# A row-normalizing kernel: the fourth load's last row and the first store's lead in 4 KB packets

## The chip, the cores and the metric

The kernel runs on one core of a Trainium2 chip. The metric is the device time of one execution in microseconds (us); the median over several runs is compared. VectorE is called DVE in the profile, ScalarE ACT, SyncE SP; "ACTq" and "SPq" are the instruction queues in which ACT and SP issue DMAs. The core has 16 DMA engines, and a DMA is cut into packets that are spread over them.

## The reference

```python
batch, seq, dim = 32, 512, 1024
x = np.random.randn(batch, seq, dim).astype(np.float32)

sums = np.sum(np.abs(x), axis=-1, keepdims=True)
out = (x / (sums + 1e-8)).astype(np.float32)
```

Each of the 32 x 512 = 16384 rows of 1024 float32 values is divided by the sum of its absolute values. The input is 67.11 MB and so is the output; every byte is read once and written once.

## The kernel before

The 16384 rows are spread over 128 partitions, 128 rows on each, and cut into 11 tiles. Tiles 0, 1 and 10 come from the first 4096 rows, where each partition owns 32 rows in a run (12, 12 and 8 of them); each of tiles 2 to 9 is a block of 1536 rows, 12 rows in a run per partition. A row is 4 KB, so a tile of 12 rows has 48 KB per partition and 6 MB in all; tile 10 has 4 MB. Four buffers (`BUFS = 4`) hold the tiles in turn, and everything is done in place in them.

For each tile `normalize` runs on DVE: a reduction of absolute values for all rows (line 47), the addition of the epsilon (54), the reciprocal (56). Then the rows are scaled in three groups, set by `split`: the first `kv` rows in one broadcast multiply on DVE (58), the next `kt` rows one by one on DVE (65), the last rows one by one on ACT (68). For tile 0 `split` is (3, 4): 5 rows in the broadcast multiply, 3 single ones on DVE, 4 on ACT.

The order is written out by hand (`manual_schedule`): SP issues loads 0 to 3; then for each tile come the computation, its store, and the load of the tile four further on. Loads go through SP's DMA queue (q1 in the profile, line 87) and stores through ACT's (q10, line 97). Load i+4 needs the buffer of tile i, so SP waits for the end of store i before it issues it; behind that wait stand only later loads. Tiles wait for one another in nothing else but the order on each engine.

`max_dma_last_dim` sets the packet size: it cuts the run of each partition into pieces. Loads 0 and 1 go in pieces of 48 KB (`WHOLE`), the others in halves of the run. Store 0 is two DMAs: rows 0 to 2 (`FIRST = 3`) in packets of one row, 4 KB, which waits for the broadcast multiply alone, then rows 3 to 11 in one packet of 36 KB per partition, which waits for all of tile 0. Store 8 is two DMAs too. The other stores are one DMA each, in packets of 24 KB, 48 KB (tile 9) or 32 KB (tile 10).

Of the kernel before, what the change touches and what calls it, by code (L numbers as in the profile page):

```python
# [1 line left out]

# [4 lines left out]

FP32 = mybir.dt.float32
EPS = 1e-8


@with_exitstack
def kernel(
    ctx: ExitStack,
    tc: tile.TileContext,
    x: bass.AP,
    out: bass.AP,
):
    nc = tc.nc
    P = nc.NUM_PARTITIONS  # L20

    x_flat = x.flatten_outer_dims()
    out_flat = out.flatten_outer_dims()
    n, d = x_flat.shape

    R = 12
    BUFS = 4
    HEAD = 32
    per_partition = n // P
    assert n % P == 0 and (per_partition - HEAD) % R == 0  # L30
    rows = [R] * ((per_partition - HEAD) // R + 2) + [HEAD - 2 * R]

    def piece(flat, i):
        head = flat[: P * HEAD, :].rearrange("(p r) d -> p r d", p=P)
        if i < 2:
            return head[:, R * i : R * (i + 1), :]
        if i == len(rows) - 1:
            return head[:, 2 * R :, :]
        a = P * (HEAD + R * (i - 2))
        return flat[a : a + P * R, :].rearrange("(p r) d -> p r d", p=P)  # L40

    sbuf = ctx.enter_context(tc.tile_pool(name="sbuf", bufs=BUFS))
    stats = ctx.enter_context(tc.tile_pool(name="stats", bufs=len(rows)))

    def normalize(x_tile, k, kv, kt):
        s = stats.tile([P, R], FP32)
        nc.vector.tensor_reduce(  # L47
            out=s[:, :k],
            in_=x_tile[:, :k, :],
            axis=mybir.AxisListType.X,  # L50
            op=mybir.AluOpType.add,
            apply_absolute_value=True,
        )
        nc.vector.tensor_scalar_add(out=s[:, :k], in0=s[:, :k], scalar1=EPS)  # L54
        inv = stats.tile([P, R], FP32)
        nc.vector.reciprocal(out=inv[:, :k], in_=s[:, :k])  # L56
        if kv:
            nc.vector.tensor_mul(  # L58
                out=x_tile[:, :kv, :],
                in0=x_tile[:, :kv, :],  # L60
                in1=inv[:, :kv].unsqueeze(2).to_broadcast([P, kv, d]),
            )
        for r in range(kv, kv + kt):
            row = x_tile[:, r, :]
            nc.vector.tensor_scalar_mul(out=row, in0=row, scalar1=inv[:, r : r + 1])  # L65
        for r in range(kv + kt, k):
            row = x_tile[:, r, :]
            nc.scalar.activation(  # L68
                out=row,
                in_=row,  # L70
                func=mybir.ActivationFunctionType.Copy,
                scale=inv[:, r : r + 1],
            )

    last = len(rows) - 1
    split = {0: (3, 4), 1: (0, 3), 2: (0, 3), last - 1: (0, 2), last: (4, 4)}

    tiles = {}

    HALF, WHOLE = 24576, 49152
    FIRST = 3

    def load(i):
        x_tile = tiles[i] = sbuf.tile([P, R, d], FP32, name="x_tile")
        nc.sync.dma_start(out=x_tile[:, : rows[i], :], in_=piece(x_flat, i), max_dma_last_dim=WHOLE if i < 2 else HALF)  # L87

    def store(i):
        if i == 0:  # L90
            parts = [(0, FIRST, 4 * d), (FIRST, R, WHOLE)]
        elif i == last - 2:
            parts = [(0, R // 2, HALF), (R // 2, R, HALF)]
        else:
            parts = [(0, rows[i], WHOLE if i >= last - 1 else HALF)]
        for a, b, size in parts:
            nc.scalar.dma_start(
                out=piece(out_flat, i)[:, a:b, :],
                in_=tiles[i][:, a:b, :],
                max_dma_last_dim=size,  # L100
            )

    def compute(i):
        k = rows[i]
        kt, ks = split.get(i, (0, 0))
        normalize(tiles[i], k, k - kt - ks, kt)

    with tc.manual_schedule():
        for i in range(BUFS):
            load(i)  # L110
        for i in range(len(rows)):
            compute(i)
            store(i)
            if i + BUFS < len(rows):
                load(i + BUFS)


# [1 line left out]
_INS = ['x']  # L119
_OUTS = [((32, 512, 1024), 'float32')]  # L120


# [23 lines left out]
```

## Time and profile before

| | |
|---|---|
| median of 3 runs | 316.62 us (316.51 to 316.66) |
| span of the profiled execution, first to last instruction | 315.2 us (315.155 in the trace) |
| median less the span | 1.46 us |
| DVE busy | 260.6 us (83%) |
| ACT busy | 18.5 us (6%) |
| moved by DMA | 134.22 MB in 5761 packets, 426 GB/s over the span |
| first packet of a load, last packet of a store | 1.73 us, ends at 313.83 us |
| first part of store 0 issued | 36.78 us |
| load 3 landed, store 0 ended | 65.86 us, 76.76 us |
| load 4 issued | 76.83 us |
| last store issued | 293.25 us |

The page gives the span of the profiled execution and no other time for it; the runs that the median comes from lie 1.46 us above this span. Times in the table, and all that are given as a moment, count from the start of the span. A packet's record in the trace holds its start, its duration, its size and its queue. The DMA row of the page gives the busy share of the 16 DMA engines in 40 equal slices, each digit a tenth.

### The profile page before, as it was taken

Reading aid. Unit: us, or ns where it says so; the run is one execution under the profiler, and the core shown is the slowest. Engines: PE = TensorE matmul, PEld = TensorE weight load, DVE = VectorE, ACT = ScalarE, POOL = GpSimd, SP = SyncE. Lnnn points to the kernel's source line nnn. Section 1 sums busy time; section 2 is a strip of 40 time slices with the busy share of each in tenths; the row PEclk is TensorE's granted clock in tenths of the full one; section 3 lists DMA queues with packets and bytes.
Section 4 is the critical chain, followed back from the end, with each engine's and each line's share of the span. In section 5 each row is a group of like instructions: output and inputs, shape, how many; then the busy total and the mean of one; then the engine's idle time right before and its main releaser. Section 6 shows DMA issues by size and latency. Waiting matters only on the chain.

```text
span 315.2 us, 172 instructions
## 1 busy us (share of the span) xinstructions
DVE 260.6 (83%) x50; ACT 18.5 (6%) x17; POOL 0.2 (0%) x4
## 2 busy tenths in 40 slices
DVE  0079999999999999989996997999699969999000
ACT  0010503004000000000000000000000000203200
POOL 0000000000000000000000000000000000000000
DMA  8999999999999999999999999999999999999997
GB/s 318 480 399 412 437 407 464 411 436 413 415 446 437 415 446 437 415 449 434 415 449 437 412 449 437 412 449 437 415 446 437 415 437 434 432 428 496 399 408 324
DMA packets 5761, 134.22 MB, mean 426 GB/s; under 512 B 385, under 2 KB 385, under 8 KB 769
## 3 DMA queue, kind: packets, MB, share of 16 engines
q1 hardware_dynamic: 2736, 67.11, 49.8%
q10 hardware_dynamic: 3024, 67.11, 49.4%
q14 instruction: 1, 0.00, 0.0%
HBM read 67.11 MB, written 67.11 MB: 426 GB/s over the span
## 4 chain that ended last, share of the span: by engine, by line
DVE 40%; DMA 33%; another core or an unknown queue 18%; ACT 1%; issue 0%; SPq 0%
DVE s L47 23%; DMA x_tile<-in_x_dram 17%; DMA out_dram<-x_tile 16%; DVE x_tile L58 15%; ACT x_tile L68 1%; DVE x_tile L65 1%; DVE inv L56 0%; DVE s L54 0%; SPq L87 0%
## 5 line engine op out<-in xcount | busy, mean ns | idle before, releaser
L47 DVE TENSOR_REDUCE s<-x_tile 128x12 f32<-128x12288 f32 (+1 forms) x11 | 138.2, 12562 | 29.8 <-DMA x_tile<-in_x_dram 29.8
L58 DVE TENSOR_TENSOR x_tile<-x_tile,inv 128x12288 f32<-128x12288 f32 (+3 forms) x10 | 113.6, 11358 | 0.5
L68 ACT ACTIVATE x_tile<-x_tile,inv 128x1024 f32<-128x1024 f32 x16 | 17.2, 1138 | 256.9 <-DVE inv L56 256.9
L65 DVE TENSOR_SCALAR x_tile<-x_tile,inv 128x1024 f32<-128x1024 f32 x7 | 4.8, 749 | 0.0
L56 DVE RECIPROCAL inv<-s 128x12 f32<-128x12 f32 (+1 forms) x11 | 2.5, 226 | 0.4
L68 ACT ACT_TABLE_LOAD x1 | 1.3, 1283 | 17.8 <-DMA x_tile<-in_x_dram 17.8
L54 DVE TENSOR_SCALAR s<-s 128x12 f32<-128x12 f32 (+1 forms) x11 | 1.9, 174 | 0.4
L130 POOL MEMSET const-bfloat16-1.0<- 128x1 bf16 x1 | 0.1, 101 | 0.0
L130 POOL MEMSET const-uint8-127<- 128x1 uint8 x1 | 0.1, 101 | 0.0
L130 POOL MEMSET const-float32-0.0<- 128x1 f32 x1 | 0.1, 98 | 0.2 <-issue 0.2
L130 POOL MEMSET const-float32-1.0<- 128x1 f32 x1 | 0.1, 98 | 0.0
## 6 DMA issues: line engine op xcount, KB each, us to landing
x_tile<-in_x_dram SPq DMA_DIRECT2D x10, 6144.0 KB, 36.9
out_dram<-x_tile ACTq DMA_DIRECT2D x8, 6144.0 KB, 49.1
out_dram<-x_tile ACTq DMA_DIRECT2D x2, 3072.0 KB, 33.4
out_dram<-x_tile ACTq DMA_DIRECT2D x1, 4608.0 KB, 37.9
x_tile<-in_x_dram SPq DMA_DIRECT2D x1, 4096.0 KB, 32.2
out_dram<-x_tile ACTq DMA_DIRECT2D x1, 4096.0 KB, 20.9
out_dram<-x_tile ACTq DMA_DIRECT2D x1, 1536.0 KB, 29.3
```

The lines of the kernel that those rows point to most:

```text
L47: nc.vector.tensor_reduce(out=s[:, :k], in_=x_tile[:, :k, :], axis=mybir.AxisListType.X, op=mybir.AluOpType.add, apply_absolute_value=True,)
L54: nc.vector.tensor_scalar_add(out=s[:, :k], in0=s[:, :k], scalar1=EPS)
L56: nc.vector.reciprocal(out=inv[:, :k], in_=s[:, :k])
L58: nc.vector.tensor_mul(out=x_tile[:, :kv, :], in0=x_tile[:, :kv, :], in1=inv[:, :kv].unsqueeze(2).to_broadcast([P, kv, d]),)
L65: nc.vector.tensor_scalar_mul(out=row, in0=row, scalar1=inv[:, r : r + 1])
L68: nc.scalar.activation(out=row, in_=row, func=mybir.ActivationFunctionType.Copy, scale=inv[:, r : r + 1],)
L130: nc = _bacc.Bacc("TRN2", target_bir_lowering=False, num_devices=1)
```

## The change

Load 3, the last of the loads that are issued at the start, becomes two DMAs: rows 0 to 10 in two packets of 22 KB per partition, and row 11 (`TAIL = 1`) in one packet of 4 KB per partition. The first part of store 0 gets four rows in 4 KB packets instead of three (`FIRST = 4`), and its second part eight rows in one packet of 32 KB per partition instead of nine in one of 36 KB. So that the first part still waits for the broadcast multiply alone, tile 0's `split` goes from (3, 4) to (2, 4): 6 rows in the broadcast multiply, 2 single ones on DVE, 4 on ACT. Nothing else changes.

```diff
     last = len(rows) - 1
-    split = {0: (3, 4), 1: (0, 3), 2: (0, 3), last - 1: (0, 2), last: (4, 4)}
+    split = {0: (2, 4), 1: (0, 3), 2: (0, 3), last - 1: (0, 2), last: (4, 4)}
...
     HALF, WHOLE = 24576, 49152
-    FIRST = 3
+    FIRST = 4
+    TAIL = 1
 
     def load(i):
         x_tile = tiles[i] = sbuf.tile([P, R, d], FP32, name="x_tile")
-        nc.sync.dma_start(out=x_tile[:, : rows[i], :], in_=piece(x_flat, i), max_dma_last_dim=WHOLE if i < 2 else HALF)
+        k = rows[i]
+        if i == BUFS - 1:
+            parts = [(0, k - TAIL, HALF), (k - TAIL, k, 4 * d)]
+        else:
+            parts = [(0, k, WHOLE if i < 2 else HALF)]
+        for a, b, size in parts:
+            nc.sync.dma_start(out=x_tile[:, a:b, :], in_=piece(x_flat, i)[:, a:b, :], max_dma_last_dim=size)
```

## The prediction

> **What bounds the kernel now.** I read the page first, then the stretches, the waits, the order of time, and last the trace's record of each DMA packet (one start and duration for each; quoted in prose). The page:
>
> ```profile
> span 315.2 us, 172 instructions
> ...
> DVE 260.6 (83%) x50; ACT 18.5 (6%) x17; POOL 0.2 (0%) x4
> ...
> DMA  8999999999999999999999999999999999999997
> ...
> DMA packets 5761, 134.22 MB, mean 426 GB/s; under 512 B 385, under 2 KB 385, under 8 KB 769
> ...
> q1 hardware_dynamic: 2736, 67.11, 49.8%
> q10 hardware_dynamic: 3024, 67.11, 49.4%
> ```
>
> No engine is busy for the whole span, but the DMA row is nines in every slice but the first and the last; the load queue (q1) and the store queue (q10) together take 99.2% of the 16 engines' time. VectorE has 17% to spare. The stretches cut where the phases change:
>
> ```profile
> 0.00:1.70 1.70, 0.00 (x0) 0.00 (x0) 0.20 (x4) 1.00 0.00 0
> 1.70:40.00 38.30, 22.10 (x8) 5.55 (x5) 0.00 (x0) 1.00 1.01 430
> 40.00:66.00 26.00, 25.90 (x5) 3.23 (x3) 0.00 (x0) 1.00 1.00 418
> 66.00:80.50 14.50, 14.40 (x4) 3.23 (x3) 0.00 (x0) 1.00 0.99 429
> 80.50:278.00 197.50, 184.59 (x29) 2.19 (x2) 0.00 (x0) 1.00 1.00 433
> ```
>
> The last two columns are DMA share and GB/s. The share is full from 1.70 us on whether only loads run (to 40), loads beside the 4 KB rows of store 0 (40 to 66), only stores (66 to 80.5) or both. The rate differs: 418 in 40 to 66, where the change works. In the packet records no engine pauses by over 0.1 us between 1.73 us and its last packet, which ends between 313.28 and 313.83. So the time is work on 16 serial engines, plus 1.73 us before and 1.3 us behind it. A wait that moves costs nothing unless both queues run empty; what counts is the time that packets take.
>
> Packet starts follow each other on one engine at 1.812 us (49152 B), 1.360 (36864 B), 0.908 (24576 B) and 0.155 (4096 B). The first two sizes of loads give (1.812 - 0.908) / 24576 = 36.8 ps per byte; what is left is 4 ns per packet whatever its size (4096 B: 0.151 + 0.004). Three things lie above this line. The first packet of each engine takes 0.43 to 1.04 us longer. 27 load packets between 38.6 and 61.3 us take 0.02 to 0.19 us longer, 0.12 us per engine. And 25 packets at the end of load 3, from 62.3 to 64.2 us, take 0.09 to 0.69 us longer than their usual 0.912: 8.77 us together, **0.55 us per engine**. No other packet is off by over 15 ns.
>
> **The change part by part.** (1) *Load 3* was 2 x 128 packets of 24576 B, 16 on each engine: 16 x 0.908 = 14.53 us. It becomes 16 of 22528 B (22528 x 36.8 ps + 0.004 = 0.833 us) and 8 of 4096 B: 13.33 + 8 x 0.155 = 14.57. That is +0.04 us, plus 5 ns for one more semaphore packet.
>
> (2) *Store 0* was 24 packets of 4096 B and 8 of 36864 B on each engine: 3.72 + 10.88 = 14.60. It becomes 32 and 8 of 32768 B (1.209 us): 4.96 + 9.67 = 14.63. That is +0.03.
>
> (3) *SP* issues a fifth DMA ahead of its first wait, about 0.4 us, at about 2.7 us. Behind it stands load 4, which isn't issued before 76.8. Hidden; bare it would cost that 0.4. The extra DMA also shifts which semaphores later DMAs reuse; each reuse waits for a DMA finished tens of us earlier. Nothing.
>
> (4) *Tile 0 on VectorE*:
>
> ```profile
> 31.26 5.49 DVE L58 TENSOR_TENSOR x_tile<-x_tile,inv 128x5120 f32<-128x5120 f32 x1
> ...
> 36.67 2.07 DVE L65 TENSOR_SCALAR x_tile<-x_tile,inv 128x1024 f32<-128x1024 f32 x3
> 36.78 2.40 ACTq L97 DMA_DIRECT2D out_dram<-x_tile  x2
> ...
> 139.13 12.95 DVE L47 TENSOR_REDUCE s<-x_tile 128x12 f32<-128x12288 f32 x1 [1.44 <-DMA x_tile<-in_x_dram]
> ```
>
> The broadcast multiply took 5.49 us for 5 rows and 9.76 for 9 (tile 1), so 1.07 per row; a single row takes 0.66. Six and two instead of five and three: +0.40 us. The first part of store 0 waits for the multiply and is issued at 37.85 instead of 36.78; the second goes from 38.8 to 39.2. Behind these two ACT has only tile 1's rows, from 52 us. Loads 2 and 3 keep the engines full until 65.9, so the later issue leaves no gap; without that cover it would cost the 1.07 us. On VectorE the 0.40 runs through tiles 1 to 4, which have no idle time, and ends in the 1.44 us wait before tile 5. Stores 1 to 3 are each issued over 10 us before their queue needs them. Zero at the end.
>
> (5) *Order within 40 to 66 us.* Packets of the two queues alternate one to one while both have work. Now 24 load packets of load 3 meet 24 store packets instead of 16, so load 3 lands later: 7 more 4 KB packets ahead of it, 1.1 us, and (1): about 67.0 instead of 65.86. Tile 3's reduction starts at 84.9, which leaves 18 us. Store 0's second part has 1.2 us less to do, so store 0 ends where it did (76.76) but for (1) and (2). Load 4 waits for that:
>
> ```profile
> SPq L87 <- DMA out_dram<-x_tile: 242.1, 8, 63.3
> ```
>
> It goes out at 76.9 instead of 76.83 and everything behind shifts alike. At the far end the last store is issued at 293.25 and its first packet runs about 303.8 (313.5 less 8 x 1.209), so nothing there becomes late.
>
> (6) *The long packets of load 3*, 0.55 us per engine. They are packets 14 to 16 of that load, where its last packets run beside the last 4 KB store packets; whatever makes them long is not named in the trace. Below: the stall and the 0.12 vanish, -0.67. Above: the changed end of load 3 brings a second stall of that size, +0.55. Nearest row: the end of load 2, also beside 4 KB stores, 0.12 at most. I take no change, because load and lead still end in the same round (about 7 + 24 = 31 of 32).
>
> (7) *4 KB loads* are in no row of this trace. Below: the 4096 B store packet, 0.155 us. Above: a short load that is lengthened as the long packets were (8.77 / 25 = 0.35 us), 8 x 0.35 = +2.8 us. I take the lower end, since 4 KB stores kept 0.155 us between loads without exception. The Trainium skill's page "DMA: Bandwidth & Descriptors" (section on the iDMA fabric) has a load stream with 4 KiB rows at 408.7 GB/s on one core, which is an estimate of 16 x 4096 / 408.7 = 160 ns per packet, and the sum would be +0.04 us more. The trace has that size for stores alone.
>
> A rule of that page speaks against the change: its bandwidth fit gives each DMA a fixed 2.0 us or so, and its rules ask for 1 MiB or more in each. By it the new 512 KB load would make the time about 318.7. The trace speaks against it here: load 1's first packet follows load 0's last after a 9 ns semaphore packet on the same engine.
>
> **Sum.** 0.04 + 0.03 + 0.01 = **+0.08 us**. The profiled span of 315.16 becomes 315.24; the median of the runs shown lies 1.46 above the span, so 316.62 becomes **316.70**. What a measurement can tell from no change is about 0.2%, 0.63 us.
>
> **Rivals.** *A: the stall at the end of load 3 goes.* Short packets end both queues in small steps. For it: long packets of loads occur only beside 4 KB stores, four fifths of their time in this one place. Against: the 4 KB stores are there before and after. Time: -0.55 + 0.08 gives 316.15; with the 0.12 too 316.03; and if the engines then end level (now 0.55 us apart) some 0.3 less, 315.73. Only the last is over 0.2%.
>
> *B: short loads beside short stores starve.* From 61 to 67 us each engine alternates 4 KB with 4 KB, and a load has 0.155 us of store to hide behind instead of 0.9. If that is too little, each of 8 packets grows. Decisive (slower by 0.63) from (0.63 - 0.08) / 8 = 0.07 us each, or from one more stall as large as the old. One more stall: 316.62 + 0.08 + 0.55 = 317.25. Half the upper end: 318.1. For it: all stalls but those at the start lie beside 4 KB packets, and their number grows from 24 to 40 per engine; in proportion the 0.67 would become 1.12, 317.15. Against: 4 KB packets themselves never stalled.
>
> *C: the extra DMA opens a gap in the load queue.* At the start first packets came 1.0 us after their issue (0.73 to 1.73). If the gap were bare that is +1.0, 317.7; but stores 0 and 1 wait in the other queue, and the DMA is issued 45 us ahead. Little.
>
> **Numbers.** Forecast as summed, give or take a quarter us: 0.52. A: 0.20 (0.12 of it over 0.2% faster). B: 0.26 (0.21 of it over 0.2% slower). C: 0.02. Faster 0.12; slower 0.23; same 0.65. The range leaves out a tenth or less on each side: 315.9 (near the far end of A) to 317.7 (between B's single stall and half its upper end).
>
> **What would show it.** Right: DMA share full through 40 to 80.5, load packets of 4096 B at 0.155 to 0.16 us, load 3 landing near 67.0, store 0's end and load 4's issue within 0.2 us of 76.8 and 76.9, tile 5's wait near 1.1, the last packet near 313.9. A shows as load 3's last packets at their plain times and load 4 out near 76.3; B as 4 KB loads well over 0.16 us, and load 4 later than 77.3. The prediction is wrong if all engines pause anywhere between 1.7 and 313 us, or if the 4 KB loads are not served in turn.

## The result and the profile after

The changed kernel takes **317.00 us** (median of 21 runs, 316.86 to 317.13) against 316.61 us before (21 runs, 316.41 to 317.00): ratio 1.0013, interval 1.0007 to 1.0019. It is slower by 0.39 us. That is inside the 0.2% that the prediction called no change, but 21 runs each resolve it. The forecast was 316.70, +0.08. The sign was right and the size too small: 317.00 lies inside the stated range, but 0.30 above the sum, just outside the quarter us to which the prediction gave 0.52.

The page of the profiled execution after (its own time 317.08 us, span 315.44):

```profile
span 315.4 us, 173 instructions
...
DVE 260.9 (83%) x49; ACT 18.5 (6%) x17; POOL 0.2 (0%) x4
...
DMA  8999999999999999999999999999999999999997
...
DMA packets 6032, 134.22 MB, mean 426 GB/s; under 512 B 400, under 2 KB 400, under 8 KB 1040
...
q1 hardware_dynamic: 2880, 67.11, 49.9%
q10 hardware_dynamic: 3152, 67.11, 49.4%
```

The DMA row still has its nines and no engine became the bound. There are 271 packets more, and q1, the load queue, has 0.1% more of the engines' time. The stretches show where:

```profile
1.70:40.00 38.30, 22.14 (x7) 5.55 (x5) 0.00 (x0) 1.00 1.01 430
40.00:66.00 26.00, 25.90 (x5) 3.23 (x3) 0.00 (x0) 1.00 0.99 406
66.00:80.50 14.50, 14.40 (x4) 3.23 (x3) 0.00 (x0) 1.00 1.03 441
80.50:278.00 197.50, 184.46 (x29) 2.19 (x2) 0.00 (x0) 1.00 1.01 433
```

The last two columns are DMA share and GB/s. Before 40 and behind 80.5 us the rate is the old one. A packet's bytes are booked at its start, so the middle two rows are best read together: 26.0 x 406 + 14.5 x 441 = 16.95 MB, against 26.0 x 418 + 14.5 x 429 = 17.09 MB before. The 0.14 MB that are missing take 0.32 us at 433 GB/s. That is a rough figure, since one packet on each engine is already 16 x 24576 B = 0.39 MB. The ends say it better: store 0 ended 0.2 us later than before (76.96 against 76.76), and the last packet also 0.2 us later (314.04 against 313.83). So the loss on the DMA engines arises ahead of 77 us, with the share full.

VectorE and the issues of store 0 went as the sum had them:

```profile
31.21 6.56 DVE L58 TENSOR_TENSOR x_tile<-x_tile,inv 128x6144 f32<-128x6144 f32 x1
...
37.69 1.41 DVE L65 TENSOR_SCALAR x_tile<-x_tile,inv 128x1024 f32<-128x1024 f32 x2
37.80 1.73 ACTq L104 DMA_DIRECT2D out_dram<-x_tile  x2
...
139.68 12.95 DVE L47 TENSOR_REDUCE s<-x_tile 128x12 f32<-128x12288 f32 x1 [1.62 <-DMA x_tile<-in_x_dram]
```

and so did the waits of SP for stores, which lead to the next loads:

```profile
SPq L94 <- DMA out_dram<-x_tile: 241.6, 8, 64.2
```

In the packet records (start and duration of each) the plain times give +0.06 us per engine. The load packets that take longer than usual, each engine's first left out, add up to 0.93 us per engine instead of 0.69. 0.80 of the 0.93 sit in packets 9 to 16 of load 3's first part, from 55 to 63 us, the longest in packets 15 and 16.

### The profile page after: what moved, and what is told of

Same layout as the page of the kernel before. It is cut to its first block, busy times and chain, and to the rows that moved or that the text cites. A ratio compares the mean times of both kernels' runs of the same rounds, so it can differ in the third digit from the quotient of the medians.

```text
span 315.4 us, 173 instructions
## 1 busy us (share of the span) xinstructions
DVE 260.9 (83%) x49; ACT 18.5 (6%) x17; POOL 0.2 (0%) x4
## 4 chain that ended last, share of the span: by engine, by line
DVE 37%; DMA 33%; another core or an unknown queue 18%; issue 3%; ACT 1%; SPq 0%
DVE s L47 23%; DMA x_tile<-in_x_dram 17%; DMA out_dram<-x_tile 15%; DVE x_tile L58 13%; ACT x_tile L68 1%; DVE inv L56 0%; DVE x_tile L65 0%; DVE s L54 0%; SPq L94 0%
## 5 line engine op out<-in xcount | busy, mean ns | idle before, releaser
L65 DVE TENSOR_SCALAR x_tile<-x_tile,inv 128x1024 f32<-128x1024 f32 x6 | 4.1, 748 | 0.0
```

## The experiments

Three numbers of each run tell its parts. "Long" is the time by which load packets exceed the usual one of their size (first packet of each engine left out), per engine, from the packet records of the one profiled execution. "Outside" is the time from the last landing to the end of the timed run: from the last landing to the last instruction in the profile, plus the median by which a run's time exceeds its span. "Records" is the number of VectorE's instructions in the trace, waits and drains among them.

| run | median us | ratio to before | records | outside us | long us |
|---|---|---|---|---|---|
| before | 316.61 | | 64 | 2.62 | 0.69 |
| after | 317.00 | 1.0007 to 1.0019 | 64 | 2.64 | 0.93 |
| tail_only | 317.38 | 1.0013 to 1.0031 | 65 | 3.00 | 0.95 |
| lead4_only | 316.88 | 1.0000 to 1.0017 | 63 | 2.78 | 0.59 |
| split_only | 316.69 | 0.9993 to 1.0010 | 63 | 2.77 | 0.37 |
| no_lead | 317.05 | 1.0002 to 1.0020 | 63 | 2.83 | 0.99 |
| split_aligned | 316.56 | 0.9990 to 1.0008 | 64 | 2.60 | 0.52 |
| tail_split | 317.13 | 1.0008 to 1.0026 | 64 | 2.66 | 0.91 |
| two_ends | 316.63 | 0.9994 to 1.0012 | 64 | 2.62 | 0.58 |
| tail8k | 317.07 | 1.0005 to 1.0023 | 64 | 2.63 | 0.67 |
| tail_first | 316.90 | 1.0001 to 1.0020 | 64 | 2.62 | 0.79 |
| load3_16k | 316.92 | 1.0003 to 1.0021 | 64 | 2.62 | 0.91 |
| load3_48k | 316.69 | 0.9997 to 1.0015 | 64 | 2.57 | 0.60 |
| lead12k | 317.63 | 1.0012 to 1.0032 | 64 | 2.57 | 0.63 |

Each but the first two has 11 runs. The runs of before in the three groups had medians of 316.63, 316.59 and 316.60.

### The parts of the change one by one

**tail_only**: the changed kernel with store 0 and tile 0 as before.

```diff
-    split = {0: (2, 4), 1: (0, 3), ...
+    split = {0: (3, 4), 1: (0, 3), ...
-    FIRST = 4
+    FIRST = 3
```

> Only load 3 is cut (11 rows in 22 KB packets, one row in 4 KB packets); store 0 and tile 0 stay as before. Theory T (the cut of load 3, its 22 KB pieces and its second end, lengthens load 3's packets): packet work +0.05 us, long packets of load 3 about 0.80 us per engine instead of 0.55, sum +0.3: 316.9 to 317.0. Theory L (the longer lead of 4 KB stores does it): +0.05 alone, long packets 0.55 us, 316.65. Theory S (both together, by ending in the same round): 316.65 too, so that this run and the next one together tell it.

Measured 317.38, outside what any theory gave: more than the whole change. The long packets are 0.95 in all, but not as theory T had it: load 3's own are 0.53, as before (0.56), and 0.41 are those of load 2, nearly all from 38 to 48 us. And 0.38 us of the 0.75 lie outside the DMA work: VectorE's drain at the end comes 0.87 us behind the last landing instead of 0.41 (before), and a run's time exceeds its span by 1.78 instead of 1.64.

**lead4_only**: the kernel before with four rows in the lead.

```diff
-    split = {0: (3, 4), ...
+    split = {0: (2, 4), ...
-    FIRST = 3
+    FIRST = 4
```

> Only store 0 and tile 0 are changed (four rows in 4 KB packets, then eight; split 6, 2 and 4); load 3 stays one DMA of 24 KB packets. Theory T: +0.03 us, long packets of load 3 0.55 us per engine, 316.65. Theory L: long packets about 0.80 us per engine, 316.9 to 317.0. Theory S: 316.65.

Measured 316.88, with 0.59 us of long packets: not longer than before. Of the 0.25 us, 0.16 are outside again. Theory L falls: the fourth lead row doesn't lengthen the load packets, though here, by the count of packets, load 3 ends some 9 lead packets before the lead does.

**split_only**: the kernel before with tile 0 as 6, 2 and 4 rows and no DMA changed.

```diff
-    split = {0: (3, 4), ...
+    split = {0: (2, 4), ...
```

> Only tile 0's split is changed (6 rows in the broadcast multiply, 2 single, 4 on ACT); no DMA differs, the first store goes out 1.07 us later and VectorE's chain of tiles 1 to 4 by 0.40 us. All theories: the time of before within 0.1 us, since the DMA engines are full. If the later issue costs, 316.62 plus up to 1.07.

Measured 316.69, as expected. But it is made of two opposite parts: the spans are 0.3 us shorter (median 314.7 against 315.0), and the time outside the span is 0.3 us longer (1.96 against 1.64).

**no_lead**: store 0 in one DMA of 24 KB packets.

```diff
-            parts = [(0, FIRST, 4 * d), (FIRST, R, WHOLE)]
+            parts = [(0, R, HALF)]
```

> Store 0 is one DMA in 24 KB packets, issued when tile 0 is done (about 38.8 us); no 4 KB packet is left anywhere. If long packets of load 3 come from 4 KB stores beside it, they vanish: -0.67 us and -0.10 for 24 packets fewer by 0.004 us net of 8 added, about 315.85 to 315.95. If they belong to the end of load 3 beside any store, they stay and the time is 316.5. Load 3 lands near 76.5 us, still ahead of its reduction at 84.9; if that were late, VectorE's chain would shift, which the 1.44 us wait before tile 5 and the later ones take up.

Measured 317.05. That is above both forecasts, with 0.21 us of it outside. With no 4 KB packet left, the long packets are more than in any other profile: 0.99 us per engine, nearly all of it from 39.6 to 44.2 us, where the stores begin, and none at the end of load 3. So 4 KB stores aren't needed for long load packets, and these don't belong to the end of load 3.

### The time outside, and which part of the cut costs

In the first four runs the time outside went with the length of VectorE's instruction stream: the dropped single-row multiply takes one away (63), and a load cut in two adds one, since tile 3's reduction must then wait for two DMAs (65). In the change both happen, and it stays at 64. no_lead has 63 because VectorE has one wait less ahead of tile 4's multiply. The second group tests that and takes the cut apart.

**split_aligned**: split_only with one single row in tile 1.

```diff
-    split = {0: (3, 4), 1: (0, 3), ...
+    split = {0: (2, 4), 1: (1, 3), ...
```

> As split_only (tile 0 scaled as 6, 2 and 4 rows), with tile 1 scaled as 8 rows, 1 single and 3 on ACT, so that VectorE's stream has 64 records in the trace again, as before, instead of 63. DMAs are those of before. Theory V (the time outside the DMA work goes by the length of VectorE's instruction stream: 2.62 us from the last landing to the end of the timed run at 64 records, 2.78 at 63, 3.00 at 65): 2.62 again, and the run keeps split_only's shorter span, so 316.69 - 0.16 = 316.53. Rival (the 0.16 us goes with the split of tile 0 in another way): 316.69.

Measured 316.56 and 2.60 us outside. Theory V held by the time outside, 2.60 for split_only's 2.77; the medians alone, 0.13 us apart, are too close to tell it from its rival.

**tail_split**: the changed kernel with three lead rows.

```diff
-    FIRST = 4
+    FIRST = 3
```

> The change without the fourth lead row: load 3 cut into 11 rows and 1, tile 0 as 6, 2 and 4 rows, store 0 as three rows and nine. VectorE's stream has 64 records. Theory V: tail_only's 317.38 less 0.38 (its 65 records) and about 0.1 for the later first store: 316.9 to 317.0. Rival (all of tail_only's 0.75 us belongs to the cut load): 317.3.

Measured 317.13 and 2.66 us outside, so the time outside is as V had it; the time of the run lies between V's 316.9 to 317.0 and its rival's 317.3. Beside split_aligned, of the same group and the same 64 records, the cut of load 3 costs 0.57 us.

**two_ends**: load 3 as two DMAs of six rows, all in 24 KB packets.

```diff
-    FIRST = 4
-    TAIL = 1
+    FIRST = 3
+    TAIL = 6
...
-            parts = [(0, k - TAIL, HALF), (k - TAIL, k, 4 * d)]
+            parts = [(0, k - TAIL, HALF), (k - TAIL, k, HALF)]
```

> Load 3 as two DMAs of six rows, both in 24 KB packets; FIRST stays 3, tile 0 as 6, 2 and 4 rows; VectorE's stream has 64 records. No 4 KB or 22 KB load packet. Theory E (a second end of a load beside 4 KB stores lengthens load packets): the longest load packets now also around the end of the first half (near 55 us), +0.35 us over split_aligned, 316.9. Theory P (the 22 KB pieces and 4 KB packets do it): as split_aligned, 316.5.

Measured 316.63. Theory E falls: with a second DMA and a second end of the load the median is 0.07 us above split_aligned's, inside the intervals. There are long packets near the end of the first half (52.5 to 54.8 us), but they come to 0.07 us per engine, and the longest are still the last ones (62.3 to 63.7 us). What is left as the cost is the sizes.

**tail8k**: ten rows in 20 KB packets, two rows in 8 KB packets.

```diff
-    FIRST = 4
-    TAIL = 1
+    FIRST = 3
+    TAIL = 2
...
-            parts = [(0, k - TAIL, HALF), (k - TAIL, k, 4 * d)]
+            parts = [(0, k - TAIL, HALF), (k - TAIL, k, 8 * d)]
```

> Load 3 as ten rows in 20 KB packets and two rows in one 8 KB packet per partition; FIRST stays 3, tile 0 as 6, 2 and 4 rows; VectorE's stream has 64 records. Theory E: +0.35 over split_aligned, 316.9. Theory P: between, by the smaller cut into odd sizes, +0.04 of packet work and half the long time, 316.7.

Measured 317.07: as dear as the 22 KB and 4 KB cut, with no 4 KB load in it, and more than theory P gave it. Its profiled execution was 0.24 us above its median and had one load packet 0.45 us too long at 129.9 us on one engine, so its 0.67 of long packets is not a good measure of the other runs.

### Short pieces or a short end

**tail_first**: tail_split with the single row issued first.

```diff
-            parts = [(0, k - TAIL, HALF), (k - TAIL, k, 4 * d)]
+            parts = [(k - TAIL, k, 4 * d), (0, k - TAIL, HALF)]
```

> As tail_split (load 3 as eleven rows in 22 KB packets and one row in 4 KB packets, FIRST 3, tile 0 as 6, 2 and 4 rows), but the single row is issued ahead of the eleven. VectorE's stream has 64 records. Theory P1 (load packets shorter than 24 KB between 4 KB stores run longer, wherever the single row stands): 317.1 as tail_split, long packets 0.8 us per engine at the last 22 KB packets. Theory P2 (the short packets at the end of the load queue do it): 316.6, long packets near 0.5.

Measured 316.90, between the two, and in a place that neither named. The stretches of tail_first, and behind them those of after, with GB/s last:

```profile
44.00:48.00 4.00, 4.00 (x1) 0.00 (x0) 0.00 (x0) 1.00 0.93 321
58.00:66.00 8.00, 8.00 (x2) 0.00 (x0) 0.00 (x0) 1.00 1.00 429
```

```profile
44.00:48.00 4.00, 4.00 (x1) 0.00 (x0) 0.00 (x0) 1.00 0.90 374
58.00:66.00 8.00, 8.00 (x2) 0.00 (x0) 0.00 (x0) 1.00 1.00 381
```

The weak stretch moved from 58 to 66 to 44 to 48 us. (Over 4 us, one packet more or less on each engine, 0.39 MB, is already 98 GB/s; the packet records decide.) In them, 0.70 of tail_first's 0.79 us are packets 15 and 16 of load 2, from 45.0 to 46.7 us, just ahead of the short row. The end of load 3, where before and after have their longest packets, has none, and all its 22 KB packets kept to their usual 0.836 us: the long ones came ahead of the first change in the load queue, which here is the short row. (split_aligned has 0.40 of its 0.52 us ahead of 55 us too, with no such change, so this is a pattern and no rule.)

**load3_16k** and **load3_48k**: split_aligned with load 3 in other packet sizes, one DMA, no single row.

```diff
-... max_dma_last_dim=WHOLE if i < 2 else HALF)
+... max_dma_last_dim=WHOLE if i < 2 else 16384 if i == 3 else HALF)
```

> split_aligned with load 3 as one DMA in three 16 KB packets per partition instead of two of 24 KB; no single row, one end. P1: 24 packets per engine instead of 16 give +0.03 us and the long packets grow at least as with 22 KB and 20 KB: +0.4 or more over split_aligned's 316.56, 317.0 or later. P2: +0.03 alone, 316.6.

```diff
-... max_dma_last_dim=WHOLE if i < 2 else HALF)
+... max_dma_last_dim=WHOLE if i < 2 or i == 3 else HALF)
```

> split_aligned with load 3 in one 48 KB packet per partition, 8 on each engine. P1: packet work -0.03 us and the long packets shrink, down to nothing: 316.1 to 316.5. P2: 316.5. Rival: fewer, longer turns leave more of the 4 KB lead behind load 3, which costs nothing as long as the engines are full.

Measured 316.92 and 316.69; long packets 0.91 and 0.60. Smaller pieces alone, with no short row and no second DMA, cost about what the change costs, which speaks for P1. Larger ones gain nothing, against P1's other half. So the long time isn't proportional to the number of packets: in the kernels with a 4 KB lead it is 0.37 to 0.69 with load 3 in 24 or 48 KB pieces and 0.67 to 0.95 with smaller ones, with one profile each.

**lead12k**: split_aligned with the lead of store 0 in 12 KB packets.

```diff
-            parts = [(0, FIRST, 4 * d), (FIRST, R, WHOLE)]
+            parts = [(0, FIRST, FIRST * 4 * d), (FIRST, R, WHOLE)]
```

> split_aligned with the first part of store 0 in one 12 KB packet per partition (8 on each engine instead of 24 of 4 KB); load 3 as before in 24 KB packets. If long load packets come from 4 KB stores beside them: they shrink, -0.5 us, and 16 packets fewer give -0.07: 316.0 to 316.1. If they come with any store that starts beside the loads (no_lead had 0.99 us of them from 39.7 to 44 us with 24 KB stores): 0.5 to 1.0 us, 316.5 to 317.0.

Measured 317.63, above both forecasts, but from 316.41 to 317.78: three of eleven runs lie at 316.62 or below, and the profiled one (316.50) is among them. In that profile the long packets, 0.63 us, run nearly all from 39.5 to 42.3 us, at the start of the stores, as in no_lead. What makes the other runs 0.5 to 1.2 us longer no profile here shows. (The interval in the table goes by the mean, 1.0022, and the median lies above it.)

No version beat the kernel before clearly; split_aligned is level with it.

## Why the prediction was right or wrong

**The bound** held in every run that was profiled: the 16 DMA engines are full from 1.7 to nearly 314 us. Moving VectorE's work alone (split_only, split_aligned) left the end of the DMA work, a median less the time outside, at 313.92 and 313.96 us for 313.99 before.

**(1) and (2), the packets**: +0.08 forecast, +0.06 in the records. **(3), the fifth DMA on SP**: issued at 2.77 us, hidden. two_ends, with a further DMA in packets of unchanged size, is 0.07 us above split_aligned, which is not clear of noise. The fixed 2.0 us per DMA, which the Trainium skill's page "DMA: Bandwidth & Descriptors" (section "Anatomy of one DMA", a fit for DMAs from GpSimd, which the prediction took for every DMA) gives, isn't seen here, where SP issues the load and packets of other DMAs follow without a gap.

**(4), tile 0**: the multiply took 6.56 us, the store went out at 37.80 for a forecast of 37.85, and the reduction of tile 1 began 0.40 us later counted from the landing of load 0. split_only, which holds this step alone, is at 1.0001, and split_aligned, which holds it with VectorE's stream at its old length, at 0.9999. The wait before tile 5 became 1.62 instead of the forecast 1.1: load 5 landed at 139.65 instead of 139.11, more than the 0.2 us by which store 0 ended later. It cost nothing.

**(5), the order**: load 3 landed at 67.28 (forecast 67.0), store 0 ended at 76.96 (76.84), load 4 went out at 77.04 (76.91), and the last packet ended at 314.04 (313.91). All are late by 0.1 to 0.3 us, which is what (6) left out. The alternation held: between 48 and 60 us after, 192 packets of loads and 192 of stores ran.

**(6), the long packets, was the term that was mis-sized.** Its change was taken as zero and measured +0.24 us (0.69 to 0.93, profile against profile; before's are packets 15 and 16 of load 3, and not 14 to 16). Its reason, that load and lead still end in the same round, carries nothing: lead4_only breaks that round and has no longer packets, tail_split breaks it and has 0.91. The cut of load 3 into packets under 24 KB goes with it (tail_only, tail_split, load3_16k, all 0.91 to 0.95), not the lead and not the second DMA. The medians say it more firmly than one profile each: less the time outside, the DMA work ends at 313.92 to 314.12 us in the six kernels with a 4 KB lead and load 3 in pieces of 24 or 48 KB, and at 314.28 to 314.47 in the six with smaller pieces. (no_lead, at 314.22, and lead12k, at 315.06, have another lead.) But how small pieces do it isn't shown: in tail_first they kept their plain times to within 0.01 us per engine, and load 2's 24 KB packets ran long. The bound above, one more stall of 0.55 us, held. With (1) and (2) this makes 0.30 us; the profiled spans differ by 0.28 and the medians by 0.39. The last 0.1 us is within what one profile can stand off: before's profiled span, 315.16, lies 0.15 above the 315.0 of its other runs, and for the same reason a run exceeds its span by 1.64 us and not by the 1.46 that the prediction used.

**(7), 4 KB loads**: 126 of 128 took the 0.159 us of the 4 KB stores, one 0.167 and one 0.308, so the lower bound was right and rival B's mechanism, starved short loads, did not appear. The prediction's estimate of 160 ns, from the Trainium skill's page "DMA: Bandwidth & Descriptors" (section on the iDMA fabric), lies within 1 ns of that.

**Rival A** (the stall goes) did not come about; **rival B** got about half of its extra stall, by 22 KB packets and not by 4 KB ones, and its argument that all stalls lie beside 4 KB packets fell with no_lead; **C** did not come about. **Not in the sum at all** was the end of the program. The change happened to leave VectorE's stream at 64 records; with only one of its two edits there the end of the program would have cost 0.16 (lead4_only) or 0.38 us (tail_only) more. That the total came out near the sum is in part this luck.

What stays open: why groups of load packets run 0.4 to 1.0 us long in sum. In most profiles it is mainly one group, in tail_only and split_aligned two. It mostly stands ahead of a change of the traffic: at the start of the stores in no_lead and lead12k and mostly in split_aligned, at the end of load 3 in before, after and most others with a 4 KB lead (with load 2's packets ahead of it in tail_only), at the end of load 2 with the short row put first. The length of VectorE's stream, store 1's issue (62.31 us in after, behind the start of its longest packets at 61.0) and the number of DMAs are excluded; the mechanism isn't shown.

## What to carry to other kernels

Where the DMA engines are full from end to end, price an edit by its packets alone, and expect packet order and size to shift a few tenths of a microsecond of long load packets about, which no sum of plain durations gives. Keep the bulk packets' size when a short piece is split off: a second DMA with equal packets cost nothing clear of noise, while cuts that made the rest 22 KB or 20 KB went with 0.3 to 0.6 us. When tenths count, compare variants only at equal length of the engines' instruction streams; here it was VectorE's that told.

## What the runs showed of the hardware that I had not expected

What the end of the program costs goes with the length of VectorE's instruction stream, far from the work itself: from the last landing to the end of the run 2.57 to 2.66 us in all ten kernels with 64 records, 2.77 to 2.83 in the three with 63, and 3.00 in the one with 65. In the records it is VectorE that comes late: at 64 its last semaphore event starts 0.96 us behind the landing where those of the other engines start at 0.75 or 0.76 (before), at 65 its drain is 0.45 us late, and at 63 it isn't late inside the span, while more time lies behind the span (1.96 instead of 1.64 us). So in all eleven profiles that have a 64th record it is this record that comes late, whichever instruction it is, and none behind it. A pause to fetch instructions would look like this. The Trainium skill's page "Runtime: NRT & Kernel Launch" (Instruction fetch mechanics) has instructions fetched in blocks, with the crossing mostly hidden; here 0.2 to 0.4 us show, but no run shows a fetch in the pause: the one 8 KB instruction packet near the end of each trace starts 0.3 to 1.1 us behind the span, so behind the late record.

Load packets ran 0.4 to 1.0 us long per engine in all 14 kernels, nearly all of it beside the first stores of the execution. In the steady state behind 80 us, where both queues carry mostly 24 KB packets, they kept their usual time (0.912 us at 24 KB) but for ten packets in four of the 14 profiles.
